# Transposing the gated product of three SwiGLU FFNs by DMA, as two planes of 16 bits, in place of TensorE

## The chip, the cores and the metric

The kernel runs on one core of a Trainium2 chip. The metric is the device time of one execution in microseconds (us): the median of three runs, 1262.65 us (1261.54 to 1262.88). One further execution was recorded by the hardware profiler; all durations below come from that one. Its span is 1259.9 us, and its granted TensorE clock 0.998 of full speed. Lines (L...) are those of the kernel before, unless the changed kernel is named.

## What is computed

Two layers over 256 latent tokens of width 1024, with 256 context tokens run through the same weights. Layer 0 is half-step FFN, neighbourhood attention, half-step FFN; layer 1 is half-step FFN, short gated convolution, half-step FFN. The last three FFNs, which the change concerns, work on the latent tokens alone. The output is the latent stream. All weights are float32.

```python
def swiglu_ffn(h, w_in, w_out):                 # w_in 1024 x 5632, w_out 2816 x 1024
    a, u = jnp.split(h @ w_in, 2, axis=-1)
    return (jax.nn.silu(a) * u) @ w_out

def half_step_ffn(x, shift, scale, gate, w_in, w_out, g, b):
    y = swiglu_ffn(modulate(x, shift, scale), w_in, w_out)
    return post_norm_update(x, y, gate, 0.5, g, b)   # layer_norm(alpha * x + 0.5 * gate * y)
```

shift, scale and gate come from a matrix-vector product of the condition c with `ada_w` (9 vectors per layer).

## The kernel before

**Precision.** A float32 product is made of three matmul passes over operands that are split in a high part (`...h`, rounded to the matmul's format) and a low part (`...l`, the remainder): high by high, low weights by high, high by low (`mmu`, L160 to 167; the rows L164, L165 and L167 of the profile are the three). ScalarE makes the high part by a copy, VectorE the low part by a subtraction.

**Weights.** A weight unit is 512 KB. `wunit` (L179) has SyncE (SP) load it into a raw tile (`w1r` for the first GEMM of an FFN, two DMAs of 256 KB; `w2r` for the second, one DMA of 512 KB; 4 raw buffers), ScalarE copies the high part in two halves of 128x512 (L210) and VectorE subtracts the low part in two halves (L213). High and low tiles have 5 buffers, and from the second phase on `ext[0]` more (L195 to 201): 3, so 8 units can be split ahead of their last use by TensorE. SP, ScalarE, VectorE and GpSimd each work through their own queue in a fixed order that a scheduler writes when the program is built; TensorE's order is written out by hand. An instruction that waits holds up all that stands behind it on its queue.

**An FFN.** `ffn` (L825) runs 11 panels (`panels`, L449). A panel is 256 gate columns and 256 up columns: 4 weight units, each used for both token tiles (t = 0, 1), so 8 steps on TensorE. Each step ends with `tick` (L143), which counts steps, runs the work whose due step has come (`Late`), and starts background work: the ada vectors of layer 1, in pieces of one DMA of 512 KB (`ar`, L303) and VectorE multiply-adds (`acc`, L296), at a rate of 0.35 per step in the first of the three FFNs, 0.25 in the second, 0.15 in the third.

When a panel's sums for one tile are done, `done` in `gated` (L475) has ScalarE write Silu of the gate half out of PSUM to `sil` (128x256, L478) and VectorE multiply it in place by the up half (L479). Rows of `sil` are tokens; the second GEMM needs columns of tokens. So at t == 1 a `Late` of `G_LAG = 4` steps follows: TensorE transposes four blocks of 128x128 (L487) into a PSUM bank `gT`, and `finish` splits that bank into `gh` on ScalarE (L112) and `gl` on VectorE (L113).

The second GEMM (`out_gemm`) runs 22 units `w2r`, tile 1 trailing tile 0 by 5 units (`order_skew`, L493), and ends in LayerNorm; the next FFN's or mixer's first units are loaded and split meanwhile.

**Where they lie.** The three FFNs take about 592 to 780 us, 781 to 965 us and 1065 to 1253 us of the span; in each the panels are the first 120 us or so, the second GEMM the rest. The first FFN of the kernel (both streams, L679), the attention and the short convolution are not touched; the convolution calls `gated` too (`uT`) and keeps its transposes on TensorE.

Of the kernel before, what the change touches and what calls it, by code (L numbers as in the profile page):

```python
# [8 lines left out]

F32 = mybir.dt.float32  # L10
F32R = mybir.dt.float32r
AF = mybir.ActivationFunctionType
ALU = mybir.AluOpType
AX = mybir.AxisListType
# [2 lines left out]
P = 128  # L17
# [34 lines left out]
LT_LAG = (5, 5)  # L52
F0_LAG = (5, 5, 6, 7)
G_LAG = 4
ROPE_EARLY = 70
S_EARLY = 40
V_LAG = 1
# [13 lines left out]
def backbone_kernel(  # L71
# [6 lines left out]
    nc = tc.nc  # L78
    sync = nc.sync
# [4 lines left out]
    sp = ctx.enter_context(tc.tile_pool(name="sp", bufs=2))  # L84
# [3 lines left out]
    hp = phase.__enter__()  # L88
# [3 lines left out]
    ext = [1, 0]  # L92
    ada_late = [0]

    def nm(s):
        uid[0] += 1
        return f"{s}_{uid[0]}"

    def act(dt=F32, s="a"):
        return ap.tile([P, 512], dt, tag="act", name=nm(s))  # L100
# [4 lines left out]
    def mmb(s="mm", t=0):  # L105
        return bank("at" if t % 2 else "mm", s)

    def tpb(s="tp"):
        return bank("tp", s)

    def split(src, hi, lo):
        a = nc.scalar.activation(hi, src, AF.Copy)  # L112
        return a, nc.vector.tensor_tensor(out=lo, in0=src, in1=hi.bitcast(F32), op=ALU.subtract)  # L113
# [42 lines left out]
    def drain():  # L156
        while background[0] is not None:
            bg_step()
# [20 lines left out]
    def wunit(srcs, kn, s, own=None, wd=512, put_off=False):  # L179
# [4 lines left out]
        if own:  # L184
            hs, ls = ([act(F32R, s + c) for _ in range(kn)] for c in "hl")
            rv = raw[:, :kn * 512].rearrange("p (a b) -> p a b", a=kn)
            with tc.high_priority(offset=w_early[0]):
                for src, c in srcs:
                    sync.dma_start(rv[:, :, c:c + src.shape[2]], src)
                for i in range(kn):  # L190
                    with queued(own[i]):
                        nc.scalar.activation(hs[i], rv[:, i], AF.Copy)
                        nc.vector.tensor_tensor(out=ls[i], in0=rv[:, i], in1=hs[i].bitcast(F32), op=ALU.subtract)
            return Parts(hs), Parts(ls)
        ext[1] += 1  # L195
        if ext[0] and ext[1] % (5 + ext[0]) in (E0 if ext[0] == 1 else E2):
            hi = hp.tile([P, UN], F32R, tag="whx", bufs=ext[0], name=nm(s + "h"))
            lo = hp.tile([P, UN], F32R, tag="wlx", bufs=ext[0], name=nm(s + "l"))
        else:
            hi = wp.tile([P, UN], F32R, tag="wh", bufs=WB[1], name=nm(s + "h"))  # L200
            lo = wp.tile([P, UN], F32R, tag="wl", bufs=WB[2], name=nm(s + "l"))
        rv, hv, lv = (t[:, :kn * wd].rearrange("p (a b) -> p a b", a=kn) for t in (raw, hi, lo))
# [4 lines left out]
        def parts():  # L207
            m = kn * wd
            for a in range(0, m, m // W_HI):
                nc.scalar.activation(hi[:, a:a + m // W_HI], raw[:, a:a + m // W_HI], AF.Copy)  # L210
            for a in range(0, m, m // W_LO):
# [35 lines left out]
    nc.scalar.dma_start(crow[8:16], c_ctx.rearrange("(a b) -> a b", b=P))  # L247
    nc.scalar.activation(warm, warm, AF.Silu)
    b0 = [[mmb("f0", z) for z in range(2)] for _ in range(3)]
# [8 lines left out]
    nc.tensor.transpose(pt[:, 0:16], crow, ident[0:16, 0:16])  # L258
    nc.scalar.activation(cst[:, :, 0:2], pt[:, 0:16].rearrange("p (v k) -> p k v", v=2), AF.Silu)
    nc.vector.memset(ones, 1.0)  # L260
# [114 lines left out]
    def queued(ins):  # L375

        es = ExitStack()
        for i in ins:
            es.enter_context(tc.issue_after(i.ins))
        return es  # L380
# [29 lines left out]
    def modulated(z, mv, rs, GB, lag, ahead=False):  # L410
# [4 lines left out]
        def rest():  # L415
            G, B = GB.get()
            res = []
            for h in range(2):
# [4 lines left out]
                with tc.high_priority(offset=LN_EARLY):  # L423
                    hi, lo = act(F32R, "hTh"), act(F32R, "hTl")
                    for k in range(4):
                        s, c = slice(k * P, (k + 1) * P), slice(4 * h + k, 4 * h + k + 1)
                        nc.scalar.activation(t[:, s], ps[:, s], AF.Identity, bias=B[:, c], scale=G[:, c])
                    ins = split(t, hi, lo)
# [13 lines left out]
    def lead_in(np):  # L442

        r = range(KU)
        o = [(0, 0, u) for u in r] + [(0, 1, u) for u in r[:2]] + [(1, 0, u) for u in r] + [(1, 1, u) for u in r[:2]]
        o += [(t, 1, u) for u in r[2:] for t in range(2)]
        return o + [(t, p, u) for p in range(2, np) for u in r for t in range(2)]

    def panels(cols, w, hTs, order, done, s, own=()):  # L449


        units, banks = {(0, u): x for u, x in enumerate(own)}, {}
        for t, p, u in order:
            if (p, u) not in units:
                with ExitStack() as st:
                    for i in fence if p == 1 else first_mv if own and p == 0 else ():
                        st.enter_context(tc.issue_after(i))
                    units[p, u] = wpair(w, u, *cols[p], s)
            if (t, p) not in banks:
                banks[t, p] = mmb(s, t)  # L460
            hi, lo = units[p, u]
            mmu(banks[t, p], [(*hsl(hTs[t], UK * u + i), hi[:, i], lo[:, i]) for i in range(UK)], u == 0, u == KU - 1)
            if u == KU - 1:
                done(p, t, banks.pop((t, p)))
            yield
            tick()

    def run(gen):
        for _ in gen:
            pass  # L470

    def gated(func, finish, s):

        part, res = {}, []

        def done(p, t, bk):
            g = sp.tile([P, 256], F32, tag="s2", bufs=S2, name=nm("sil"))
            nc.scalar.activation(g, bk[:, 0:256], func)  # L478
            gate_ins[:] = [nc.vector.tensor_tensor(out=g, in0=g, in1=bk[:, 256:512], op=ALU.mult)]  # L479
            part[p, t] = g  # L480
            if t == 1:
                def rest():
                    ps = tpb(s)
                    for i in range(2):
                        g = part.pop((p, i))
                        for j in range(2):
                            nc.tensor.transpose(ps[:, j * 256 + i * P:j * 256 + (i + 1) * P], g[:, j * P:(j + 1) * P], ident)  # L487
                    return finish(p, ps)
                res.append(Late(G_LAG, rest))

        return done, res
# [209 lines left out]
    for q, (k0, n) in enumerate(steps):  # L701
        nxt = start_step(*steps[q + 1]) if q < 4 else iter(())
        for g in range(6 * n):
# [3 lines left out]
            if k < KC - 1:  # L707
                z, part = ZP[g % 6]
# [16 lines left out]
    for fh, (p0, p1) in enumerate(parts):  # L725
        gT = []
# [90 lines left out]
    def lhs_T(tl):  # L817
        def f(k, t):
            s = (k % 2) * 256 + t * P
            g = tl[k // 2]  # L820
            hi, lo = g.get() if isinstance(g, Late) else g
            return hi[:, s:s + P], lo[:, s:s + P]
        return f

    def ffn(hTs, later, l, j, i, gm, nxt, own=()):  # L825
        def finish(p, ps):
            hi, lo = act(F32R, "gh"), act(F32R, "gl")
            split(ps, hi, lo)
            return hi, lo

        done, gT = gated(AF.Silu, finish, "gT")

        def done2(p, t, bk):
            done(p, t, bk)
            if p == 1 and t == 1:
                later()

        run(panels([(p * 256, FF + p * 256) for p in range(NP)], ffn_w_in[l, j], hTs, lead_in(NP), done2, "w1", own))
        drain()
        g, hTs, later = sub_end(ffn_w_out[l, j], lhs_T(gT), 2 * NP, l, i, gm, 0.5, nxt, "w2",  # L840
                                order_skew(NP) if nxt else order_last(NP))
        run(g)
        return hTs, later
# [45 lines left out]
    def tile_panel(c0, c1, hl, s, each):  # L889

        units = []
        for t, hT in enumerate(hl):
            bk = mmb(s)
            for u in range(KU):
# [4 lines left out]
                if u == KU - 1:  # L899
                    with tc.high_priority(offset=ROPE_EARLY):  # L900
                        each(t, bk)
# [124 lines left out]
    hp = phase.__enter__()  # L1026
# [35 lines left out]
    for i in range(len(steps) + LAG + V_LAG):  # L1062
# [14 lines left out]
        n = int(credit)  # L1077
# [12 lines left out]
        j = i - LAG - V_LAG  # L1090
# [15 lines left out]
    phase = tc.tile_pool(name="ph2", bufs=1)  # L1106
    hp = phase.__enter__()
    bias_rows.clear()
    ext[0] = 3

    set_background(stream([(1, 4, 0), (1, 5, 0)]), 0.35, HOLD)
    hTs, later = ffn(hTs, later, 0, 1, 2, 8, (1, 0), own)
# [15 lines left out]
    w = sc_w_in[0]  # L1128
# [22 lines left out]
    def done(p, t, bk):  # L1151
        if p >= 2:
            return cdone(p, t, bk)
        b = sp.tile([P, 512], F32, tag="s2", bufs=S2, name=nm("bs"))
        nc.scalar.activation(b, bk, AF.Copy)
        bs[p, t] = b
        if t == 1:
            for j in range(2):
                def rest(j=j):
                    ps = tpb("bT")  # L1160
                    for i in range(2):
                        for t in range(2):
                            nc.tensor.transpose(ps[:, i * 256 + t * P:i * 256 + (t + 1) * P],
                                                bs[p, t][:, (2 * j + i) * P:(2 * j + i + 1) * P], ident)
                    b = act(F32, "bT")
                    nc.scalar.activation(b, ps, AF.Copy)
                    return b
                bT[2 * p + j] = Late(G_LAG, rest)
            if p == 1:
                later()  # L1170
# [3 lines left out]
    g, hTs, later = sub_end(sc_w_out[0], lhs_T(yT), KC, 1, 1, 5, 1.0, (1, 6), "wo", order_late(KU))  # L1174
# [57 lines left out]
```

## Time and profile before

| | |
|---|---|
| runs, median (lowest, highest) | 1262.65 us (1261.54, 1262.88) |
| span of the profiled execution | 1259.9 us |
| TensorE (PE) busy | 1245.4 us, 99% |
| VectorE (DVE) busy | 952.5 us, 76% |
| ScalarE (ACT) busy | 589.9 us, 47% |
| GpSimd (POOL) busy | 41.4 us, 3% |
| moved by DMA | 268.59 MB, mean 213 GB/s |

The median of the runs is 2.75 us above the span of the profiled execution. PE is the row of the matmuls themselves; the loads of their stationary operand (PEld) run beside it. Busy time of PE counts overlapping matmuls as they were pipelined, so what a matmul costs in time is read from the start of one to the start of the next. In rows of groups the columns are: line, engine, operation, tiles written and read, shapes, count, then busy us in all and mean ns of one, then the idle time before them with what ended it.

### The profile page before, as it was taken

How to read it: one execution, taken by the hardware profiler on the slowest of the kernel's cores; microseconds unless marked ns; L12 is line 12 of the kernel's file. 1: busy time of each engine (PE TensorE's matmuls, PEld its weight loads, DVE VectorE, ACT ScalarE, POOL GpSimd, SP SyncE). 2: the span in 40 equal slices, each digit the busy share in tenths (PEclk: the TensorE clock that was granted, in tenths of full speed). 3: DMA queues.
4: the chain of work that ended last, by engine and by line, in shares of the span. 5: the costliest groups of instructions: out<-in, count | busy, mean ns of one | idle time of the engine just before them, and what ended most of it. 6: DMA issues, size and time to landing. Idle time of an engine off the chain costs nothing.

```text
span 1259.9 us, 17303 instructions
## 1 busy us (share of the span) xinstructions
PE 1245.4 (99%) x5922; PEld 1007.2 (80%) x5922; DVE 952.5 (76%) x1678; ACT 589.9 (47%) x1152; POOL 41.4 (3%) x71
## 2 busy tenths in 40 slices
PE   9999999999999999999999999999999999999997
PEld 6787778777878877877888788888788887888786
DVE  3699987888878877889898546988546788876546
ACT  2432132312326456687655435655435644655431
POOL 0000000000001011121000000000000000000000
PEclk9999999999999999999999999999999999999999
DMA  9976678878842744465899645898645764886641
GB/s 300 310 241 215 197 239 280 269 255 266 300 149 85 217 93 92 93 130 170 256 342 318 225 144 169 285 340 268 214 145 170 247 202 131 262 289 184 223 158 55
DMA packets 202776, 268.59 MB, mean 213 GB/s; under 512 B 30090, under 2 KB 149362, under 8 KB 202688
## 3 DMA queue, kind: packets, MB, share of 16 engines
q1 hardware_dynamic: 202652, 267.48, 67.3%
q8 instruction: 46, 0.75, 0.2%
q14 instruction: 42, 0.34, 0.1%
q10 hardware_dynamic: 36, 0.02, 0.0%
HBM read 265.27 MB, written 2.17 MB: 212 GB/s over the span
## 4 chain that ended last, share of the span: by engine, by line
PE 92%; DVE 3%; ACT 3%; issue 1%; DMA 0%; POOL 0%; DVEq 0%; SPq 0%; ACTq 0%; POOLq 0%
PE f L679 19%; PE w L164 17%; PE w L167 17%; PE w L165 17%; PE wkv L164 2%; PE wkv L165 2%; PE wkv L167 2%; PE wc L164 2%; PE wc L167 2%; PE wc L165 2%; PE gT L487 1%; PE ada L608 1%; PE ada L327 1%; PE S L971 1%; ACT pr L979 1%
## 5 line engine op out<-in xcount | busy, mean ns | idle before, releaser
L210 ACT ACTIVATE w1h<-w1r 128x512 fp32r<-128x512 f32 (+1 forms) x352 | 199.8, 620 | 180.4 <-DMA w1r<-in_ffn_w_in_dram 73.3
L213 DVE TENSOR_TENSOR w1l<-w1r,w1h 128x512 fp32r<-128x512 f32 (+1 forms) x352 | 222.9, 679 | 44.6 <-ACT w1h L210 43.3
L164 PE MATMUL w<-w1h,hTh 128*128 128x512 f32 x528 | 209.4, 397 | 0.9 <-ACT hTh L112 0.9
L165 PE MATMUL w<-w1l,hTh 128*128 128x512 f32 x528 | 206.0, 390 | 0.2 <-DVE w1l L213 0.2
L296 DVE SCALAR_TENSOR_TENSOR acc<-ar,cst,acc 128x512 f32<-128x512 f32 x266 | 186.0, 746 | 15.4 <-DMA ar<-in_ada_w_dram 15.4
L164 PE MATMUL w<-w2h,gh 128*128 128x512 f32 (+1 forms) x446 | 173.4, 389 | 0.0
L165 PE MATMUL w<-w2l,gh 128*128 128x512 f32 (+1 forms) x446 | 172.1, 386 | 0.0
L213 DVE TENSOR_TENSOR w2l<-w2r,w2h 128x512 fp32r<-128x512 f32 x176 | 114.3, 688 | 76.0 <-ACT w2h L210 75.2
L210 ACT ACTIVATE w2h<-w2r 128x512 fp32r<-128x512 f32 x176 | 101.6, 624 | 146.0 <-PE w L167 103.6
L167 PE MATMUL w<-w1h,hTl 128*128 128x512 f32 x528 | 163.2, 390 | 0.3 <-DVE hTl L113 0.2
L167 PE MATMUL w<-w2h,gl 128*128 128x512 f32 (+1 forms) x446 | 136.1, 386 | 0.0
L679 PE MATMUL f<-h0h,w1h 128*128 128x512 f32 x352 | 133.3, 394 | 0.4 <-DVE h0h L634 0.4
L679 PE MATMUL f<-h0l,w1h 128*128 128x512 f32 x352 | 133.2, 391 | 0.0
L679 PE MATMUL f<-h0h,w1l 128*128 128x512 f32 x352 | 132.7, 390 | 0.0
L164 PEld LDWEIGHTS w<-w1h,hTh 128*128 128x128 f32 x528 | 99.2, 188 | 23.8 <-ACT hTh L112 1.7
L167 PEld LDWEIGHTS w<-w1h,hTl 128*128 128x128 f32 x528 | 98.9, 188 | 22.4 <-DVE hTl L113 1.5
L165 PEld LDWEIGHTS w<-w1l,hTh 128*128 128x128 f32 x528 | 99.2, 188 | 20.2 <-DVE w1l L213 0.6
L164 PEld LDWEIGHTS w<-w2h,gh 128*128 128x128 f32 x446 | 83.8, 188 | 19.2 <-issue 1.7
L165 PEld LDWEIGHTS w<-w2l,gh 128*128 128x128 f32 x446 | 83.8, 188 | 16.6
L167 PEld LDWEIGHTS w<-w2h,gl 128*128 128x128 f32 x446 | 83.3, 188 | 17.1
L679 PEld LDWEIGHTS f<-h0h,w1h 128*128 128x128 f32 x352 | 65.9, 189 | 18.8 <-issue 4.2
L679 PEld LDWEIGHTS f<-h0l,w1h 128*128 128x128 f32 x352 | 65.6, 188 | 14.3 <-issue 0.6
(186 smaller groups left out, 1684.5 us busy)
## 6 DMA issues: line engine op xcount, KB each, us to landing
w1r<-in_ffn_w_in_dram SPq DMA_DIRECT2D x340, 256.0 KB
ar<-in_ada_w_dram SPq DMA_DIRECT2D x128, 512.0 KB
w2r<-in_ffn_w_out_dram SPq DMA_DIRECT2D x88, 512.0 KB
ar<-in_ada_w_dram SPq DMA_DIRECT2D x32, 256.0 KB
wkvr<-in_na_w_qkv_dram SPq DMA_DIRECT2D x32, 256.0 KB
wcr<-in_sc_w_in_dram SPq DMA_DIRECT2D x32, 256.0 KB
wqr<-in_na_w_qkv_dram SPq DMA_DIRECT2D x8, 512.0 KB
wor<-in_na_w_out_dram SPq DMA_DIRECT2D x8, 512.0 KB
```

Of the source, the lines that this page charges most:

```text
L164: nc.tensor.matmul(ps, lh, rh, start=first and i == 0, stop=False)
L165: nc.tensor.matmul(ps, lh, rl, start=False, stop=False)
L167: nc.tensor.matmul(ps, ll, rh, start=False, stop=last and i == n - 1)
L210: nc.scalar.activation(hi[:, a:a + m // W_HI], raw[:, a:a + m // W_HI], AF.Copy)
L213: nc.vector.tensor_tensor(out=lo[:, a:b], in0=raw[:, a:b], in1=hi[:, a:b].bitcast(F32), op=ALU.subtract)
L296: nc.vector.scalar_tensor_tensor(out=a, in0=src, scalar=sc, in1=a, op0=ALU.mult, op1=ALU.add)
L327: nc.tensor.matmul(ps[32 * j:32 * j + 32, :], ones, acc[i][h], start=True, stop=True)
L487: nc.tensor.transpose(ps[:, j * 256 + i * P:j * 256 + (i + 1) * P], g[:, j * P:(j + 1) * P], ident)
L608: nc.tensor.matmul(ps[o:o + 32, 0:m], cst[:, a * kt + i, :], w[:, i, j, :], start=(a == 0 and i < 2), stop=(a == last and i >= kt - 2))
L679: nc.tensor.matmul(ps, w, hT0[k][part == 1], start=(k == part == 0), stop=(k == KC - 1 and part == 1))
L971: nc.tensor.matmul(banks[i], (qh, qh, ql)[f][ps, qs], (kh, kl, kh)[f][ps, :], start=f == 0, stop=f == 2)
L979: nc.scalar.activation(pr, S, AF.Exp, bias=mx[:, 0:1], accum_out=mx[:, 1:2])
```

## The change

In the three FFNs of the second phase (`by_dma`), per panel and tile: behind the gate multiplication ScalarE copies the product, read as 16-bit halves, into a tile `hal` with all low halves in one plane and all high halves in the other (128x512 elements of 16 bits, 2 buffers; L486 of the changed kernel). SP issues one transposing DMA from `hal` to half of `halT` (4 blocks of 128x128 of 16 bits, 128 KB; 2 buffers; L487 there). At t == 1 a `Late` of `D_LAG = 8` steps follows: ScalarE joins the two planes into a float32 tile `gTw` in SBUF (1024 elements of 16 bits per partition; L491 there), and the same `finish` splits `gTw` (L114 and L115 there) instead of a PSUM bank. The room for the new tiles comes from the split weights: `ext[0]` goes from 3 to 2, so 7 units instead of 8 can be split ahead.

In counts: 132 transposes leave TensorE; 66 copies and 33 joins are added on ScalarE, 66 transposing DMAs on SP. The splits of `gT`, 33 on ScalarE and 33 on VectorE, stay in number.

```diff
+D_LAG = 8
...
-    def gated(func, finish, s):
+    def gated(func, finish, s, by_dma=False):
...
             g = sp.tile([P, 256], F32, tag="s2", bufs=S2, name=nm("sil"))
             nc.scalar.activation(g, bk[:, 0:256], func)
             gate_ins[:] = [nc.vector.tensor_tensor(out=g, in0=g, in1=bk[:, 256:512], op=ALU.mult)]
+            if by_dma:
+                if t == 0:
+                    part[p] = hp.tile([P, 4, 256], U16, tag="halT", bufs=2, name=nm("halT"))
+                halves = hp.tile([P, 2, 256], U16, tag="hal", bufs=2, name=nm("hal"))
+                nc.scalar.activation(halves, g.bitcast(U16).rearrange("p (f s) -> p s f", s=2), AF.Copy)
+                sync.dma_start_transpose(part[p][:, :, t * P:(t + 1) * P], halves.rearrange("p s f -> p (s f)"))
+                if t == 1:
+                    def joined():
+                        w = sp.tile([P, 512], F32, tag="tmp", bufs=3, name=nm("gTw"))
+                        nc.scalar.activation(w.bitcast(U16).rearrange("p (f s) -> p s f", s=2),
+                                             part.pop(p).rearrange("p (s j) n -> p s (j n)", s=2), AF.Copy)
+                        return finish(p, w)
+                    res.append(Late(D_LAG, joined))
+                return
             part[p, t] = g
...
-        done, gT = gated(AF.Silu, finish, "gT")
+        done, gT = gated(AF.Silu, finish, "gT", True)
...
-    ext[0] = 3
+    ext[0] = 2
```

The order on ScalarE in the panels of the first of the three FFNs, before, from one split of a transposed product (`gh<-gT`) to the next. `w1h` is the high part of a weight unit, `sil` the activated gate half; numbers behind names are running numbers of tiles.

```order
L112 ACTIVATE gh_1165_6232<-gT_1164_6227 128x512
L210 ACTIVATE w1h_1207_6440<-w1r_1206_6439 128x512 x2
L210 ACTIVATE w1h_1214_6474<-w1r_1213_6473 128x512 x2
L478 ACTIVATE sil_1175_6286<-w1_1159_6198 128x256
L478 ACTIVATE sil_1176_6295<-w1_1160_6205 128x256
L210 ACTIVATE w1h_1217_6495<-w1r_1216_6494 128x512 x2
L210 ACTIVATE w1h_1223_6526<-w1r_1222_6525 128x512 x2
L112 ACTIVATE gh_1187_6345<-gT_1186_6340 128x512
```

The same stretch of ScalarE's queue in the changed kernel, from one join to the next:

```order
L491 ACTIVATE gTw_1187_6303<-halT_1160_6182 128x2x512
L114 ACTIVATE gh_1188_6305<-gTw_1187_6303 128x512
L212 ACTIVATE w1h_1218_6439<-w1r_1217_6438 128x512 x2
L212 ACTIVATE w1h_1225_6467<-w1r_1224_6466 128x512 x2
L480 ACTIVATE sil_1184_6296<-w1_1171_6217 128x256
L486 ACTIVATE hal_1186_6300<-sil_1184_6296 128x512
L480 ACTIVATE sil_1190_6315<-w1_1172_6224 128x256
L212 ACTIVATE w1h_1229_6492<-w1r_1228_6491 128x512 x2
L486 ACTIVATE hal_1191_6318<-sil_1190_6315 128x512
L212 ACTIVATE w1h_1232_6513<-w1r_1231_6512 128x512 x2
L491 ACTIVATE gTw_1212_6420<-halT_1185_6299 128x2x512
```

The first `hal` stands directly behind its `sil`, whose VectorE multiplication lies between them; the second has the two halves of one weight unit between. From the second `hal` to the join of the same panel (`halT_1185`) there stand the two halves of one weight unit.

SP's queue in that stretch, before: loads of weight units and of ada pieces alone.

```order
L205 DMA w1r_1199_6411<-in_ffn_w_in_dram 128x2x256 x2
L205 DMA w1r_1206_6439<-in_ffn_w_in_dram 128x2x256 x2
L205 DMA w1r_1213_6473<-in_ffn_w_in_dram 128x2x256 x2
L303 DMA ar_1171_6267<-in_ada_w_dram 128x1024
L303 DMA ar_1181_6314<-in_ada_w_dram 128x1024
L205 DMA w1r_1216_6494<-in_ffn_w_in_dram 128x2x256 x2
```

SP's queue there in the changed kernel, with the two transposes of one panel:

```order
L207 DMA w1r_1217_6438<-in_ffn_w_in_dram 128x2x256 x2
L487 DMA_TRANSPOSE halT_1160_6182<-hal_1161_6183 128x4x128
L207 DMA w1r_1224_6466<-in_ffn_w_in_dram 128x2x256
L487 DMA_TRANSPOSE halT_1160_6182<-hal_1166_6201 128x4x128
L305 DMA ar_1180_6277<-in_ada_w_dram 128x1024
L305 DMA ar_1196_6337<-in_ada_w_dram 128x1024
```

Each transpose waits on SP for its `hal`, and the loads behind it wait with it. The order of the matmuls themselves is the same in both kernels, without the four `gT` transposes between two steps.

More of the change, by code (lines that the diff above doesn't have):

```diff
@@ L11 @@
 F32R = mybir.dt.float32r
+U16 = mybir.dt.uint16
 AF = mybir.ActivationFunctionType
```

## The prediction, made before the changed kernel ran

> **What bounds the kernel now.** I read first the page's chain of the work that ended last, to see which engine an edit must touch to move the end.
>
> ```profile
> span 1259.9 us, 17303 instructions
> PE 92%; DVE 3%; ACT 3%; issue 1%; DMA 0%; POOL 0%; DVEq 0%; SPq 0%; ACTq 0%; POOLq 0%
> PE f L679 19%; PE w L164 17%; PE w L167 17%; PE w L165 17%; PE wkv L164 2%; PE wkv L165 2%; PE wkv L167 2%; PE wc L164 2%; PE wc L167 2%; PE wc L165 2%; PE gT L487 1%; PE ada L608 1%; PE ada L327 1%; PE S L971 1%; ACT pr L979 1%
> ```
>
> TensorE carries 92% of the chain, and the transposes of the product (`gT L487`) stand on it themselves. Then I read the chain in order of time inside a panel (start, length, what), to price them where they stand.
>
> ```profile
> 642.72 0.46 PE w L167 x2
> 643.17 0.44 PE gT L487 x4
> 643.61 0.24 PE w L164
> ...
> 654.07 0.46 PE w L167 x2
> 654.53 0.44 PE gT L487 x4
> ```
>
> One panel is 654.53 − 643.17 = 11.36 us, of which the four transposes delay the next matmul by 0.44 us; nothing in it waits. Without them TensorE needs 10.92 us. Third, the busy times by stretch: start and end, then busy us of PE, PEld, DVE, ACT and POOL, the clock, the DMA share and GB/s. The first is early in the panels of the first FFN, the second later in them, the third its second GEMM, the last the third FFN's panels.
>
> ```profile
> 620.00:640.00 20.00, 20.00 (x93) 16.55 (x93) 17.56 (x31) 10.45 (x20) 0.00 (x0) 1.00 0.81 274
> 640.00:660.00 20.00, 20.00 (x93) 16.54 (x93) 20.00 (x35) 11.35 (x23) 0.00 (x0) 1.00 0.98 336
> 740.00:760.00 20.00, 20.00 (x90) 16.55 (x89) 12.57 (x21) 8.07 (x14) 0.00 (x0) 1.00 0.59 198
> 1120.00:1140.00 20.00, 20.00 (x93) 16.55 (x92) 15.56 (x26) 10.58 (x20) 0.00 (x0) 1.00 0.70 217
> ```
>
> TensorE is full in all, but VectorE and the DMA engines are full too at 640 us (20.00 of 20; 0.98). ScalarE has 8.65 us of 20 free there, which is what the change spends. What protects TensorE is the stock of split weight units. The groups by line give it, from 585 us to 611 us and to 660 us: one unit is two ScalarE halves and four matmuls of L164.
>
> ```profile
> L210 ACT ACTIVATE w1h<-w1r 128x512 fp32r<-128x512 f32 x19 | 11.0, 646 | 7.0 <-POOL rs L403 3.0 <-PE wo L167 1.9 <-DMA w1r<-in_ffn_w_in_dram 1.2
> L164 PE MATMUL w<-w1h,hTh 128*128 128x512 f32 x26 | 10.3, 398 | 0.2 <-ACT hTh L112 0.2
> ...
> L164 PE MATMUL w<-w1h,hTh 128*128 128x512 f32 x94 | 37.3, 397 | 0.2 <-ACT hTh L112 0.2
> ...
> L210 ACT ACTIVATE w1h<-w1r 128x512 fp32r<-128x512 f32 x58 | 33.4, 631 | 26.6 <-DMA w1r<-in_ffn_w_in_dram 13.8 <-PE w L167 4.7 <-DVE w1l L213 3.1
> ```
>
> By 611 us, where the first `gT` stood, 9.5 units are split and 6.5 used: 3 ahead; by 660 us 29 and 23.5: 5.5 ahead. A unit is two steps, 10.92 / 4 = 2.73 us. One unit is in hand, so the reserve at the first transpose is about 2 x 2.7 = 5.4 us.
>
> **The change part by part.** *TensorE's transposes go.* 33 groups of 0.44 us are 14.5 us, all on the chain. The row of the matmuls themselves says otherwise, and must not be used:
>
> ```profile
> L487 PE MATMUL gT<-ident,sil x132: 270/272/273, 611.6 to 1196.3; 128*128 128x128 f32 x132
> ```
>
> Each lasts 272 ns, but four start within 0.44 us, 110 ns apart. The Trainium skill ("TensorE: Matmul & The Clock Gate", Part 4: PE-mode transpose) gives some 275 ns for a transpose in a kernel's context. By it, taken as a price each, 132 would give 36.3 us and a forecast 21.8 us lower; the trace agrees with the duration, not with such a price. I take −14.5 us, also the most that can be won.
>
> *ScalarE's new work.* Rows of the first FFN's panels, ScalarE and VectorE:
>
> ```profile
> L210 ACT ACTIVATE w1h<-w1r 128x512 fp32r<-128x512 f32 x76 | 43.5, 628 | 32.3 <-PE w L167 14.4 <-DMA w1r<-in_ffn_w_in_dram 13.5 <-DVE w1l L213 3.1
> L478 ACT ACTIVATE sil<-w 128x256 f32<-128x256 f32 x21 | 7.9, 381 | 10.7 <-PE w L167 10.7
> L112 ACT ACTIVATE gh<-gT 128x512 fp32r<-128x512 f32 x10 | 5.9, 591 | 3.3 <-PE gT L487 3.3
> L479 DVE TENSOR_TENSOR sil<-sil,w 128x256 f32<-128x256 f32 x21 | 8.6, 416 | 3.3 <-ACT sil L478 3.3
> L296 DVE SCALAR_TENSOR_TENSOR acc<-ar,cst,acc 128x512 f32<-128x512 f32 x28 | 19.5, 745 | 0.0
> L213 DVE TENSOR_TENSOR w1l<-w1r,w1h 128x512 fp32r<-128x512 f32 x78 | 49.5, 686 | 10.1 <-ACT w1h L210 10.0
> ```
>
> No row shows a 16-bit copy. A `hal` has the 512 elements of a half unit: 0.63 us. Between 256 and 512 elements ScalarE takes (628 − 381) / 256 = 0.96 ns each, so a join of 1024 takes 0.63 + 512 x 0.96 ns = 1.12 us. Should 16 bits go at half the price, both are 0.3 and 0.6; at double, 1.25 and 2.2; I take the rows' rate, as the instructions are otherwise copies of the same kind. `gh` then reads SBUF, 0.63 for 0.59.
>
> *The path that matters* is ScalarE's queue around the join. Work per panel: four units (two halves start to end take 1.15 us, row below) 4.60, two `sil` 0.76, two `hal` 1.26, join 1.12, `gh` 0.63: 8.37 us, under 10.92, so the work alone fits. To it come two waits. The first `hal` stands directly behind its `sil`, so ScalarE waits for VectorE's 0.42 us, or 1.17 with an `acc` of 0.75 ahead of it: 0.8. And it waits at the join for the transpose: T from the end of the second `hal`, less what stands between (one unit in the rows shown, 1.15; two and a half at the place before it, 2.9; middle 2.0). So a panel takes ScalarE 8.37 + 0.8 + T − 2.0 = 7.2 + T.
>
> *T* is shown by no row. Bounds from issues of plain DMAs and what waited for them:
>
> ```profile
> 990.40 0.93 SPq L345 DMA_DIRECT2D lng<-in_ln_g_dram  x2
> 996.23 1.90 DVE L780 TENSOR_TENSOR x<-x,lng 128x512 f32<-128x512 f32 x3 [2.15 <-DMA lng<-in_ln_g_dram]
> 1256.41 0.99 SPq L812 DMA_DIRECT2D out_dram<-x  x2
> ```
>
> With an empty queue, the end of the span comes 1259.9 − 1257.4 = 2.5 to 3.5 us after the last store's issue; behind weight loads, 996.23 − 991.33 = 4.9 to 5.8 us pass. So T is 2.5 to 5.8 if a transpose is like a plain DMA. At DMA shares of 0.81 to 0.98 it is nearer to the second row: I take 4.4 in the first two FFNs, 3.8 in the third (share 0.70). Then ScalarE's panel is 11.6 and 11.0 us against 10.92. Ten intervals between joins cost 10 x 0.68 − 5.4 = 1.4 us in each of the first two FFNs, nothing in the third: +2.8. At T = 2.5 it is 0; at 5.8, (10 x 2.08 − 5.4) x 3 = 46 us.
>
> *The queues.* Behind a transpose on SP stand the next loads; each waits until `hal` is written. Beside the waits of ScalarE on loads this counts:
>
> ```profile
> ACT w1h L210 <- DMA w1r<-in_ffn_w_in_dram: 10.1, 6, 3.8
> ...
> ACT w1h L210 <- PE w L167: 14.4, 12, 1.6
> ```
>
> At 610 to 640 us loads come late (10.1 us in all), at 640 to 700 us buffers bound (14.4): so the reserve fills only after the first panels. The transposes add 2 x 128 KB per panel; at 336 GB/s that is 0.78 us of engines that are full at 640 us. Over four such panels in each of two FFNs that is 6.2 us, or nothing where the wait at the join covers it: half, +3.1.
>
> *FFN ends.* In the changed order a `hal` stands once per FFN ahead of the next split on the way, at most 0.63 x 3 = +1.9.
>
> *Seven units instead of eight.* In the second GEMM (ScalarE by time):
>
> ```profile
> 733.02 1.15 ACT L210 ACTIVATE w2h<-w2r 128x512 fp32r<-128x512 f32 x2 [1.59 <-PE w L167]
> 735.74 1.15 ACT L210 ACTIVATE w2h<-w2r 128x512 fp32r<-128x512 f32 x2 [1.57 <-PE w L167]
> ```
>
> A split starts when TensorE frees a buffer, every 2.72 us. Tile 1 trails by five units, so six are held and two are ahead: 5.4 − 1.15 (ScalarE) − 0.69 (VectorE) = 3.6 us of slack; with seven, 2.72 − 1.84 = 0.9. I cost it at nothing: what hides it is that ScalarE has little else (8.07 of 20). One `acc` of 0.75 in front is still covered; two are not.
>
> Sum: −14.5 + 2.8 + 3.1 + 1.9 = −6.7 us. The profiled span with the 2.75 us around it is the median, so 1262.65 − 6.7 = 1256.0 us.
>
> **The rivals.** *All is hidden.* T is 3 or so: ScalarE needs 10.2 us and never falls behind. Then 1262.65 − 14.5 = 1248.2, with FFN ends 1250. For it: ScalarE's free 8.65 us of 20. Against: shares of 0.98.
>
> *ScalarE's wait at the join sets the pace: slower.* It is the same cycle with T beyond some point, where 10 x (7.2 + T − 10.92) − 5.4 reaches the 3.2 us per FFN that are left of the gain, (14.5 − 3.1 − 1.9) / 3: that is T = 4.6. T = 5 gives 7.4 us per FFN, 22 in all: 1262.65 − 14.5 + 22 + 5.0 = 1275; T = 5.8 gives 1299. For it: the 4.9 to 5.8 us of the `lng` row, and that ScalarE's weight splits, which feed TensorE, stand behind the join. Against: when TensorE is slowed, the loads thin out and T falls. Of this rival's chance a third, 0.10, is for T of 5.2 and more: 1281 and up. Beside this stands a rule of the Trainium skill ("VectorE: DVE Perf Modes", The three transpose paths): a 128x128 transpose by DMA takes 1309 ns, and TensorE is to be used where PSUM will do. An estimate from it, four blocks one behind the other, is 5.2 us for one DMA, and so a T of at least that; no row here tells.
>
> *The transposes clog the DMA engines.* If one holds the engines for the 2.5 us of the empty-queue row, two make 5 us a panel beside 0.81 x 11.36 = 9.2 in the first FFNs and 8.0 in the third. 14.2 and 13.0 us per panel give (33 − 5.4) x 2 + (21 − 5.4) = 71 us: 1320. Another page of the Trainium skill ("DMA: Bandwidth & Descriptors", Latency and other measured facts) speaks against this with 261 GB/s for transposing DMAs, by which 128 KB take 0.5 us (an estimate).
>
> *Seven buffers bite.* Two `acc` ahead of a split in the second GEMM exceed the 0.9 us by 0.6; on 1 to 5 units of each FFN that is 2 to 9 us on top of the forecast: 1258 to 1265. VectorE's 12.57 of 20 speak against more.
>
> That the change doesn't do what it says is excluded by the order of the instructions: the matmul groups of `gT` are gone and the transposes stand on SP.
>
> **How the numbers follow.** Forecast 0.33 (own range 1250 to 1261), all hidden 0.17, wait at the join 0.30, clogged 0.12, seven buffers 0.08. A measurement here tells 0.2% from no change, 2.5 us: faster is below 1260.1, slower above 1265.2. Faster: 0.17 + 0.27 of the forecast + 0.03 of the buffers = 0.47. Same: 0.05 + 0.04 + 0.03 of the join case = 0.12. Slower: 0.27 + 0.12 + 0.01 + 0.01 = 0.41. The range runs from 1247.5 (all hidden, less the runs' scatter) to 1285 (T = 5.3 at the join); left out are the clogged case, 0.12, and 0.08 of the join case's upper end.
>
> **What would show it.** Right: panels in the changed trace of 10.92 us on PE in the third FFN, and in the first two some steps in which PE waits for ACT or DVE splits; a join on ACT that idles 2 to 3 us for a DMA; `hal` near 0.63 and the join near 1.1 us; second GEMMs with no wait. Wrong: joins that idle over 4 us and panels above 11.4 us (the slower rival); a DMA share near 0.98 in the third FFN (clogged); PE waiting in the second GEMM (buffers); no wait anywhere (all hidden).

## The result, and the profile after

The changed kernel takes 1297.19 us (median of 4 runs, 1293.82 to 1299.21) against 1262.12 us before, of which there are now four runs: the ratio is 1.0276, with a 95% interval of 1.026 to 1.0291. It is slower by 35 us, where a gain of 6.7 us was forecast. The profiled execution has a span of 1295.7 us. Its page, the span and the chain of the work that ended last:

```profile
span 1295.7 us, 17199 instructions
...
PE 58%; DMA 15%; DVE 12%; ACT 9%; issue 4%; SPq 2%; POOL 0%; DVEq 0%; ACTq 0%
PE f L695 19%; PE w L167 8%; PE w L166 8%; PE w L169 7%; DMA w1r<-in_ffn_w_in_dram 7%; DMA halT<-hal 5%; DVE w1l L215 5%; ACT w1h L212 2%; PE wc L166 2%; PE wc L167 2%; PE wc L169 2%; DMA lng<-in_ln_g_dram 1%; DVE acc L298 1%; ACT gTw L491 
```

TensorE carried 92% of the chain before and carries 58% now; the transposing DMA alone has 5%. But that does not say in which stage the time went. For this I take each stage from the first to the last start of its matmuls of high weights by high, as the view by tile gives them. For the third FFN, before and after (the first row of each pair is the second GEMM, the second the panels):

```profile
L164 PE MATMUL w<-w2h,gh x94: 278/389/474, 1191.9 to 1252.0; 128*128 128x512 f32 x82, 128*128 128x256 f32 x12
L164 PE MATMUL w<-w1h,hTh x176: 389/389/499, 1064.9 to 1191.0; 128*128 128x512 f32 x176
```

```profile
L166 PE MATMUL w<-w2h,gh x94: 278/389/795, 1215.6 to 1287.5; 128*128 128x512 f32 x82, 128*128 128x256 f32 x12
L166 PE MATMUL w<-w1h,hTh x176: 389/389/499, 1093.5 to 1214.7; 128*128 128x512 f32 x176
```

The panels are 126.1 us before and 121.1 after: the full gain of the transposes is there. The second GEMM is 60.1 before and 72.0 after. All three FFNs, in us, and the runs that are told below:

| | panels 1 | panels 2 | panels 3 | second GEMM 1 | 2 | 3 | median us |
|---|---|---|---|---|---|---|---|
| before | 126.7 | 126.3 | 126.1 | 60.8 | 60.9 | 60.1 | 1262.12 |
| changed | 125.7 | 132.2 | 121.1 | 71.9 | 71.5 | 72.0 | 1297.19 |
| e1 seven units alone | 126.7 | 125.9 | 125.9 | 60.8 | 60.9 | 60.1 | 1262.14 |
| e2 no join waits | 124.5 | 124.9 | 121.1 | 61.8 | 60.4 | 59.6 | 1252.65 |
| e3 last two panels on TensorE | 133.3 | 141.0 | 129.3 | 60.9 | 60.9 | 60.1 | 1287.75 |
| e4 joins moved | 124.3 | 131.0 | 121.1 | 63.8 | 60.4 | 59.6 | 1261.88 |
| e5 last two joins don't wait | 125.0 | 132.0 | 121.1 | 63.1 | 64.6 | 67.6 | 1274.68 |
| e6 first nine joins don't wait | 123.6 | 124.3 | 121.1 | 70.0 | 71.3 | 59.6 | 1270.83 |
| e7 plain DMA | 121.9 | 125.9 | 121.1 | 67.1 | 69.1 | 62.6 | 1268.64 |
| e8 no waits, no DMA | 122.9 | 121.2 | 121.0 | 60.3 | 60.4 | 59.6 | 1246.19 |
| e9 third FFN alone, moved | 126.7 | 125.9 | 121.1 | 60.8 | 60.8 | 59.6 | 1256.55 |
| e10 first and third, moved | 123.8 | 125.9 | 121.1 | 63.8 | 60.8 | 59.6 | 1258.80 |
| e11 moved, issued by ScalarE | 122.1 | 121.1 | 121.1 | 65.3 | 61.9 | 59.6 | 1254.04 |
| e12 third FFN alone, not moved | 126.7 | 125.9 | 121.1 | 60.9 | 60.9 | 67.9 | 1265.20 |

From before to changed the panels together are 0.1 us shorter (−1.0, +5.9, −5.0) and the second GEMMs 33.6 us longer (11.1, 10.6, 11.9). The span grew by 35.8 us: nearly all of it is in the second GEMMs. That is the net change. Without the four transposes a panel would be 0.44 us shorter, some 4.8 us per FFN, so the panels of the second FFN lost about 11 us of their own (132.2, where e8 has 121.2). (In the kernel before, the second FFN runs to about 970 us, 908.7 + 60.9, and not to 965.)

Why there? ScalarE's queue by time, in the third FFN's panels of the changed kernel (start, length, and in brackets the idle time before with what ended it):

```profile
1157.19 0.63 ACT L486 ACTIVATE hal<-sil 128x512 uint16<-128x512 uint16 x1 [1.15 <-DVE sil L481]
1157.73 0.37 ACT L480 ACTIVATE sil<-w 128x256 f32<-128x256 f32 x1
1157.99 1.14 ACT L212 ACTIVATE w1h<-w1r 128x512 fp32r<-128x512 f32 x2
1159.04 0.62 ACT L486 ACTIVATE hal<-sil 128x512 uint16<-128x512 uint16 x1
1159.56 1.14 ACT L212 ACTIVATE w1h<-w1r 128x512 fp32r<-128x512 f32 x2
1163.18 1.37 ACT L491 ACTIVATE gTw<-halT 128x1024 uint16<-128x1024 uint16 x1 [2.48 <-DMA halT<-hal]
1164.58 0.63 ACT L114 ACTIVATE gh<-gTw 128x512 fp32r<-128x512 f32 x1
1165.12 2.18 ACT L212 ACTIVATE w1h<-w1r 128x512 fp32r<-128x512 f32 x4
1167.20 0.36 ACT L480 ACTIVATE sil<-w 128x256 f32<-128x256 f32 x1
1168.71 0.63 ACT L486 ACTIVATE hal<-sil 128x512 uint16<-128x512 uint16 x1 [1.15 <-DVE sil L481]
```

From one first copy to the next are 1168.71 − 1157.19 = 11.52 us, for TensorE's 10.92. Of these ScalarE waits 1.15 us for VectorE's multiplication and 2.48 us for the transpose; the work is 7.9 us. So ScalarE falls back by 0.6 us in this panel of the lightest FFN, and TensorE lives on the stock. The eight last intervals between first copies in this FFN are 11.2 to 12.8 us. How much of it is left when the second GEMM begins is counted by the halves of `w2` split by then, before (until 1191.9 us) and after (until 1215.6 us):

```profile
L210 ACT ACTIVATE w2h<-w2r 128x512 fp32r<-128x512 f32 x14 | 8.1, 624 | 8.5 <-PE w L167 8.5
```

```profile
L212 ACT ACTIVATE w2h<-w2r 128x512 fp32r<-128x512 f32 x4 | 2.2, 617 | 0.0
```

Seven units before, two after; the other two FFNs have the same counts, 14 halves and 4. And the second GEMM starts at double pace: tile 1 trails by five units, so for its first five units TensorE takes a new one every 1.36 us. The chain by time at that point of the changed kernel:

```profile
1217.50 0.62 ACT hal L486
1218.12 0.11 ACT w2h L212
1218.23 3.25 DMA halT<-hal
...
1221.56 1.35 ACT gTw L491
...
1229.00 0.53 ACT hal L486
...
1229.55 5.36 DMA halT<-hal
...
1234.93 1.35 ACT gTw L491
...
1236.84 0.62 ACT w2h L212
```

The joins of the tenth and eleventh panel stand here ahead of the splits that TensorE waits for, and each waits for its transpose (3.25 and 5.36 us of chain). In this GEMM the starts of matmuls that lie over 0.5 us apart add up to 9.1 us of standing, and those a little apart to 3.2 us more, which is the clock (last section).

### The profile page after: what moved, and what is told of

Its sections match the earlier page's. It is cut to its first block, busy times and chain, and to the rows that moved or that the text cites. A ratio compares the mean times of both kernels' runs of the same rounds, so it can differ in the third digit from the quotient of the medians.

```text
span 1295.7 us, 17199 instructions
## 1 busy us (share of the span) xinstructions
PE 1250.8 (97%) x5790; PEld 998.6 (77%) x5790; DVE 949.6 (73%) x1678; ACT 661.0 (51%) x1251; POOL 41.8 (3%) x71
## 4 chain that ended last, share of the span: by engine, by line
PE 58%; DMA 15%; DVE 12%; ACT 9%; issue 4%; SPq 2%; POOL 0%; DVEq 0%; ACTq 0%
PE f L695 19%; PE w L167 8%; PE w L166 8%; PE w L169 7%; DMA w1r<-in_ffn_w_in_dram 7%; DMA halT<-hal 5%; DVE w1l L215 5%; ACT w1h L212 2%; PE wc L166 2%; PE wc L167 2%; PE wc L169 2%; DMA lng<-in_ln_g_dram 1%; DVE acc L298 1%; ACT gTw L491 1%; PE wkv L166 1%
## 5 line engine op out<-in xcount | busy, mean ns | idle before, releaser
L166 PE MATMUL w<-w1h,hTh 128*128 128x512 f32 x528 | 206.7, 392 | 1.7 <-ACT hTh L114 0.9
L166 PE MATMUL w<-w2h,gh 128*128 128x512 f32 (+1 forms) x446 | 178.2, 400 | 16.7 <-ACT w2h L212 16.7
L167 PE MATMUL w<-w2l,gh 128*128 128x512 f32 (+1 forms) x446 | 177.8, 399 | 3.1 <-DVE w2l L215 3.1
L169 PE MATMUL w<-w2h,gl 128*128 128x512 f32 (+1 forms) x446 | 139.6, 395 | 0.0
L169 PEld LDWEIGHTS w<-w2h,gl 128*128 128x128 f32 x446 | 85.9, 194 | 17.9
L491 ACT ACTIVATE gTw<-halT 128x1024 uint16<-128x1024 uint16 x33 | 45.1, 1367 | 73.8 <-DMA halT<-hal 73.8
```

What stands on the lines that cost most here:

```text
L166: nc.tensor.matmul(ps, lh, rh, start=first and i == 0, stop=False)
L167: nc.tensor.matmul(ps, lh, rl, start=False, stop=False)
L169: nc.tensor.matmul(ps, ll, rh, start=False, stop=last and i == n - 1)
L491: nc.scalar.activation(w.bitcast(U16).rearrange("p (f s) -> p s f", s=2), part.pop(p).rearrange("p (s j) n -> p s (j n)", s=2), AF.Copy)
```

## The experiments

Theory H: the loss is the two join waits at the hand-over from the panels to the second GEMM. Rival B: it is the buffer that was given up. Rival D: it is the traffic of the transposes. Each ratio is to runs of the kernel before that belong to the experiment; their medians lie between 1261.55 and 1262.13 us. After the first four runs H had to be widened to theory L: all eleven joins put ScalarE back, and the sum is paid where units go at double pace.

**e1: seven units alone.** The kernel before with one edit.

```diff
-    ext[0] = 3
+    ext[0] = 2
```

> The kernel before with seven split units instead of eight, nothing else. Theory H (hand-over): in the changed kernel the joins of the last two panels, each waiting on ScalarE for its transpose, stand ahead of the first splits of the second GEMM's weights, and TensorE spends its stock there at one unit per 1.36 us; that costs about 11 us per FFN. Then seven units alone cost little: 1262 to 1265 us, second GEMMs of 60.8 to 62 us. Rival B (buffers): the one unit fewer is what TensorE lacks at the start of the second GEMM; then 1285 us or more here. Rival D (DMA load): the traffic of the transposes delays the weight loads; then as under H, 1262 to 1265.

Measured: 1262.14 us, ratio 0.9999 (0.999 to 1.0008). B falls for the kernel before: there the eighth unit is worth nothing (the stock at the second GEMM is six units, 12 halves, and nothing waits). Eight units in the changed kernel were not tried. Its stock of two stands far below the limit of seven, so the limit isn't what it lacks; that is argued, not shown.

**e2: joins that don't wait.** The product used is not the real one.

```diff
-    nc.scalar.activation(w.bitcast(U16).rearrange("p (f s) -> p s f", s=2),
-                         part.pop(p).rearrange("p (s j) n -> p s (j n)", s=2), AF.Copy)
+    nc.scalar.activation(w.bitcast(U16).rearrange("p (a b) -> p a b", a=4),
+                         ident.bitcast(U16).unsqueeze(1).to_broadcast([P, 4, 256]), AF.Copy)
```

> The changed kernel with the join reading a constant tile in place of the transposed one: copies, transposing DMAs and joins all still run, but no join waits for a transpose; the product used is not the real one. H: the second GEMMs fall from 72 to 61 to 62 us, the total to 1250 to 1262 us. B: 1285 us or more, as the buffers are still seven. D: 1290 us or more, as the traffic is the same.

Measured: 1252.65 us, ratio 0.9922 (0.9906 to 0.9938). The second GEMMs are 59.6 to 61.8 us. With the same traffic and the same seven units, 44.5 us of the changed kernel's 1297.19 are gone: traffic or buffers alone don't make the loss. Such a join also takes 1.04 instead of 1.37 us, and the scheduler places it earlier: no join stands behind the start of a second GEMM here, two do in the changed kernel. So this run doesn't yet part the wait from the place of the join; e4 does.

**e3: the last two panels transposed by TensorE.**

```diff
-            if by_dma:
+            if by_dma and p < NP - 2:
```

> The changed kernel with the last two panels of each FFN transposed by TensorE as before, the first nine by DMA. H: the second GEMMs are 61 to 62 us, the total 1262 to 1270 us. B: about as the changed kernel, 1290 us or more. D: 2 of 11 of the loss comes back, about 1290 us.

Measured: 1287.75 us, ratio 1.0206 (1.019 to 1.0223). H foretold the second GEMMs (60.9, 60.9, 60.1) and missed the total by 18 us above its band: now the panels are 8 us longer than in the changed kernel. The waits in the stretch of the first FFN, and those of the third:

```profile
ACT gTw L491 <- DMA halT<-hal: 16.9, 8, 3.2
PEld gT L503 <- DVE sil L481: 6.7, 1, 6.7
```

```profile
ACT gTw L491 <- DMA halT<-hal: 18.3, 7, 3.4
...
PEld gT L503 <- DVE sil L481: 5.5, 1, 5.5
```

TensorE comes to its transposes, four steps or 5.5 us behind the sums, and the product is not there for another 5.5 to 6.7 us (8.1 in the second FFN): `sil` stands on ScalarE behind the last waiting join and the splits after it. So ScalarE's lag has built up over nine panels, and comes out wherever TensorE first needs something fresh of it. H in its narrow form falls.

**e4: joins moved.** All work as in the changed kernel; each join is ordered behind the first copy of the next panel, the last one six steps later.

```diff
+                if t == 0:
+                    behind_ins[:] = [c]          # c: the copy to hal
...
+                        with tc.issue_after((behind_ins if p < NP - 1 else hi_ins)[0].ins):
...
-                    res.append(Late(D_LAG, joined))
+                    res.append(Late(D_LAG + (6 if p == NP - 1 else 0), joined))
```

> The changed kernel with the same work, and each join placed on ScalarE behind the first copy of the next panel (the last panel's behind several splits of the second GEMM), so that the transpose has landed when its turn comes. H: no join idles over 0.5 us, the second GEMMs are 61 to 62 us, the total 1248 to 1260 us. B: 1285 us or more. D: 1290 us or more.

Measured: 1261.88 us, ratio 0.9997 (0.9987 to 1.0006): 35 us come back by order alone. ScalarE by time in the third FFN's panels:

```profile
1129.84 0.63 ACT L488 ACTIVATE hal<-sil 128x512 uint16<-128x512 uint16 x1 [0.90 <-DVE sil L483]
1130.38 1.35 ACT L496 ACTIVATE gTw<-halT 128x1024 uint16<-128x1024 uint16 x1
...
1139.50 0.63 ACT L488 ACTIVATE hal<-sil 128x512 uint16<-128x512 uint16 x1 [2.08 <-DVE sil L483]
1140.04 1.35 ACT L496 ACTIVATE gTw<-halT 128x1024 uint16<-128x1024 uint16 x1
```

No join waits in any panel, as expected, though two or three joins per FFN still stand behind the start of the second GEMM; in the second and third FFN these cost nothing. So it is the wait that costs, not the place. Two expectations were missed. The total is 2 us above the band, since the second FFN's panels still have 131.0 us; e11 takes that up. And the first FFN's second GEMM has 63.8 us for 61 to 62; it starts with 4 halves of `w2` split, the third with 12.

**e5 and e6: which joins.** The join of e2 for some panels only; the other joins wait. The same limits hold as there.

```diff
+                        if p >= NP - 2:      # e5; e6: if p < NP - 2
```

> The changed kernel; only the joins of the last two panels of each FFN read a constant tile instead of the transposed one, so these two don't wait; the first nine do. Theory H (the two waits at the hand-over are the loss): second GEMMs of 61 to 62 us, total 1262 to 1268 us. Theory L (lag: each of the eleven joins puts ScalarE back by a part of its wait, and the sum is paid where the second GEMM takes units at double pace): the lag of nine panels stays, second GEMMs of 66 to 69 us, total 1275 to 1288 us.

> The changed kernel; the joins of the first nine panels read the constant tile and don't wait, those of the last two wait for their transposes. H: the loss at the hand-over stays, second GEMMs of 70 to 72 us, total 1285 to 1292 us. L: ScalarE reaches the hand-over with a full stock and two waits of 3 to 4 us take little of it, second GEMMs of 61 to 64 us, total 1253 to 1262 us.

Measured: e5 1274.68 us (ratio 1.0101, 1.0086 to 1.0116), e6 1270.83 us (1.0071, 1.0054 to 1.0087). Over e2 the waits of the first nine joins cost 22.0 us, those of the last two 18.2, all eleven 44.5. e5 lies at the lower edge of L's band, e6 between the two bands: neither theory is right alone. The FFNs differ: in the third the last two waits cost nothing by themselves (59.6) and the nine cost 8 us (67.6); in the first two the last two waits cost 8 to 11 us by themselves (70.0, 71.3 against 61.8, 60.4). The stock says why. Halves of `w2` split when the second GEMM begins, third FFN of e5, third FFN of e6, first FFN of e6:

```profile
L212 ACT ACTIVATE w2h<-w2r 128x512 fp32r<-128x512 f32 x4 | 2.3, 617 | 0.0
```

```profile
L212 ACT ACTIVATE w2h<-w2r 128x512 fp32r<-128x512 f32 x12 | 6.9, 622 | 6.3 <-PE w L169 6.3
...
L212 ACT ACTIVATE w2h<-w2r 128x512 fp32r<-128x512 f32 x7 | 4.1, 622 | 0.7 <-DMA w2r<-in_ffn_w_out_dram 0.6
```

With 12 halves the two waits are covered; with 7, where loads come late, they are not; with 4 the GEMM stands even without them (63.1 to 67.6 us in the three FFNs of e5, with 3 to 4 halves each).

**e7: a plain DMA in place of the transposing one.** The product is not transposed.

```diff
-                sync.dma_start_transpose(part[p][:, :, t * P:(t + 1) * P], halves.rearrange("p s f -> p (s f)"))
+                sync.dma_start(part[p][:, :, t * P:(t + 1) * P], halves.rearrange("p s (j f) -> p (s j) f", j=2))
```

> The changed kernel with a plain DMA of the same bytes from the two planes to the same tile, in pieces of 256 bytes, in place of the transposing one; the product is not transposed. If transposing itself makes the DMA slow, the time from the second copy to the join falls from 3.7 to 2.5 to 3 us and the total to 1265 to 1280 us. If it is the latency of any DMA behind weight loads, it stays at 3.4 to 3.9 us and the total at 1290 us or more.

Measured: 1268.64 us, ratio 1.0057 (1.0036 to 1.0077). From the end of the second copy to the start of the join are 3.33 us on average over the 33 panels (2.2 to 5.1), against 3.76 (2.4 to 5.6) in the changed kernel. SP's issues in the two, minimum, median and longest in ns, changed kernel first:

```profile
L487 SPq DMA_TRANSPOSE halT<-hal x66: 1188/1191/1998, 604.5 to 1229.5; - x66
```

```profile
L487 SPq DMA_DIRECT2D halT<-hal x66: 593/600/681, 603.4 to 1205.0; - x66
```

The total fell as the first band had it; T lies between the two bands. But these means hold joins that didn't wait, 4 and 10 of the 33, where ScalarE's own work sets the time. For the joins that did wait, T is 3.82 us with the transposing DMA and 3.12 with the plain one. Of that, 1.51 and 0.63 us pass until SP has issued, and from there to the join 2.31 and 2.49 us. So once issued, the transposing DMA is not slower here; it comes later, by 0.6 us at the issue and the rest in SP's queue. That 0.7 us of T give 28.6 us back is not shown to be T alone, since SP is free sooner for the loads and the scheduler also put more splits between copy and join.

**e8: no waits and no transposing DMA.** e2 with the line of the DMA taken out.

> As the run whose joins read a constant tile, and the transposing DMAs left out as well: copies and joins on ScalarE alone. If the traffic of the transposes and their place in SP's queue hold up the weight loads (panels of the second FFN 124.9 us there, 121.1 in the third), these fall to 121 to 122 us and the total from 1252.7 to 1244 to 1247 us. If it is ScalarE's added work or the seven buffers, they stay, 1250 to 1253 us.

Measured: 1246.19 us, ratio 0.9877 (0.9862 to 0.9892), as expected. The second FFN's panels fall from 124.9 to 121.2 us. ScalarE's waits on weight loads, e2 first, then e8:

```profile
ACT w1h L212 <- DMA w1r<-in_ffn_w_in_dram: 92.6, 50, 5.7
```

```profile
ACT w1h L212 <- DMA w1r<-in_ffn_w_in_dram: 47.0, 32, 4.0
```

So the copies and joins as such cost nothing that shows, and the transposes' DMAs cost about 6 us (6.5 by the medians, 5.7 by the two ratios), by their traffic or by their place in SP's queue.

**e9, e10, e12: which FFNs.**

```diff
-        done, gT = gated(AF.Silu, finish, "gT", True)
+        done, gT = gated(AF.Silu, finish, "gT", nxt is None)   # e9, e12; e10: j == 1
```

> The moved joins of the run before (each behind the first copy of the next panel), with the DMA transposes in the third FFN alone; the first two are transposed by TensorE as before. In that run the third FFN had panels of 121.1 us and a second GEMM of 59.6 us, against 126.1 and 60.1 before, and the first two together lost that gain again. If the FFNs add up, 1262 - 5.5 = 1256 to 1258 us. If something else is lost with the change (the buffers, the ends of FFNs), 1260 us or more.

> The same with the first and the third FFN. With moved joins the first FFN had 124.3 and 63.8 us against 126.7 and 60.8 before: +0.6. If the FFNs add up, 1256 to 1259 us, no better than the third alone.

> The change as it was, joins not moved, in the third FFN alone. There the changed kernel's panels gained 5.0 us and the second GEMM lost 11.9: if the FFNs add up, 1262 + 6.9 = 1267 to 1271 us.

Measured: e9 1256.55 us (ratio 0.9958, 0.9945 to 0.9972), e10 1258.80 (0.9977, 0.9966 to 0.9987), both as expected. e12 gives 1265.20 (1.0026, 1.0016 to 1.0036), 2 us below its band: the second GEMM loses 7.8 us there, not 11.9, and its last join waits 2.85 us, not 5.40; why is open. Even in the FFN with the least traffic, the change with unmoved joins loses. e9 and e12 differ in nothing but the order of the joins in one FFN. Halves of `w2` split when its second GEMM begins, e9 first:

```profile
L214 ACT ACTIVATE w2h<-w2r 128x512 fp32r<-128x512 f32 x12 | 7.0, 623 | 5.4 <-PE w L169 5.4
```

```profile
L212 ACT ACTIVATE w2h<-w2r 128x512 fp32r<-128x512 f32 x5 | 2.8, 617 | 0.0
```

The second GEMM takes 59.6 us with the one, 67.9 with the other.

**e11: joins moved, transposes issued by ScalarE.**

```diff
-                sync.dma_start_transpose(part[p]...
+                nc.scalar.dma_start_transpose(part[p]...
```

> Moved joins in all three FFNs, with the transposing DMAs issued by ScalarE instead of SP, so that no weight load stands behind one. If what is still lost (panels of 131 us in the second FFN) comes from loads held up in SP's queue, these panels fall to 122 to 126 us and the total from 1262 to 1250 to 1256 us. If the traffic itself delays the loads, they stay at 129 us or more. Against either: issuing takes 1.19 us each on SP; if it takes ScalarE as long, 2.4 us a panel, ScalarE needs about 11 us a panel without any wait and the total is 1262 us or more.

Measured: 1254.04 us, ratio 0.994 (0.9926 to 0.9953): faster than both kernels, by 8 and 43 us. Issuing does take ScalarE as long (1.21 us each), but the 1262 us or more expected in that case didn't come. ScalarE's waits on weight loads in the second FFN's panels, e4 first; below it the largest row of the waits of SP's transposes there; then e11:

```profile
ACT w1h L214 <- DMA w1r<-in_ffn_w_in_dram: 32.5, 17, 4.0
```

```profile
SPq L491 <- ACT hal L488: 24.5, 8, 5.4
```

```profile
ACT w1h L214 <- DMA w1r<-in_ffn_w_in_dram: 13.8, 12, 3.7
```

The second FFN's panels fall from 131.0 to 121.1 us with the same transposes. So the loads were late because they stood behind transposes on SP, not because of the traffic. In these panels SP's transposes waited 44 us in all for ScalarE (24.5 in the row shown), and issuing 22 of them took it another 26 us; which of the two held the loads more isn't parted. This is shown for the kernel with moved joins; for the changed kernel itself, where SP's transposes waited 48 us in these panels, it wasn't tried. The first FFN's second GEMM stays at 65.3 us. It starts with four halves of `w2` and its last join waits 2.95 us, which is the picture of the changed kernel; why its stock is so short here stays open.

## Why the prediction was wrong

- **The transposes' 14.5 us** were about right: the third FFN's panels are 5.0 us shorter, and with all else hidden (e8) the ratio of 0.9877 is 15.5 us.
- **ScalarE's work**: the copy was right, the join was not, 1.37 us for the 1.12 forecast:

```profile
L486 ACT ACTIVATE hal<-sil x66: 613/630/667, 603.8 to 1228.9; 128x512 uint16<-128x512 uint16 x66
...
L491 ACT ACTIVATE gTw<-halT x33: 1342/1368/1387, 614.8 to 1234.9; 128x1024 uint16<-128x1024 uint16 x33
```

- **T** was within its bounds, and the value taken (4.4 and 3.8) was above the measured 3.87, 3.70 and 3.71 in the three FFNs. **ScalarE's panel** was to be 7.2 + T: 10.7 for the 3.52 us of the panel shown, where 11.52 were measured. The 0.8 us are the join (+0.25), the first copy's wait (1.15 for 0.8, +0.35) and the one unit between copy and join, where the middle of one and two and a half was taken (+1.0); 0.7 us come off, since instructions of ScalarE overlap at their ends.
- **The step that failed** is the reserve: "10 x 0.68 − 5.4 = 1.4 us". It let the panels spend the stock of split units, took what was spent for free, and put the second GEMM's loss at nothing. The panels did spend it and lost nothing in the third FFN. But the second GEMM needs this stock. It was priced from rows of its steady state (a split every 2.72 us, ScalarE 8.07 of 20 busy), where nothing presses; its first five units go at 1.36 us, with two joins still to come on ScalarE's queue. Seven units stood ready before, two now, and the three second GEMMs lost 33.6 us. That the waits at the joins spend the stock, and that the stock is what the second GEMM lacks, is shown by e4, and by e9 beside e12: the same work with the joins moved leaves six units in the third FFN, and its second GEMM loses nothing.
- **The signs.** A join that idles 2 to 3 us, taken as a sign of the forecast, came (2.24 us on average). TensorE waiting in the second GEMM came too, but it was taken as a sign of too few buffers; e1 speaks against that reading.
- **Seven units, the ends of FFNs**: e1 shows no cost of the buffer, as forecast; the +1.9 us of the ends can't be told from the noise of the stages.
- **The queues** were named and sized at +3.1, too little: e2 against e8 gives about 6 us, e4 against e11 7 to 8 us, most of it in the second FFN's panels.
- **The rivals**: the wait at the join was the right mechanism and the wrong threshold. It was to decide from T = 4.6; it decided at 3.76, since the price falls due at the hand-over and not in the panels. The rule behind the rival (the Trainium skill, "VectorE: DVE Perf Modes", Rules for kernel authors: TensorE where PSUM will do) came out right for the changed kernel and not for e11, where the DMA path is 8 us faster than TensorE's. The price beside the rule did not come out: four blocks at 1309 ns one behind the other are 5.2 us, the estimate of the prediction, and here copy to join takes 3.76 us for all four, latency included. The clogged engines didn't come: the DMA share in the third FFN's panels was 0.82.

## What to carry to other kernels

A stock that is built up ahead of an engine isn't free to spend: find the next place where it is drawn faster than it is filled, and price the change there, from rows of that place. When a transfer is put between two operations of one in-order engine, place the second one where the transfer has landed anyway: moving the joins was worth 35 us at equal work. And look at what stands behind a DMA that waits for its source: issuing it from the engine that writes the source took 7 to 8 us off here.

## What was not expected of the hardware

The idle stretches cost more than their length, since the granted clock fell after them. Windows of the changed kernel (the number after the engines is the granted clock):

```profile
738.00:741.00 3.00, 1.01 (x4) 0.34 (x2) 0.94 (x4) 2.97 (x5) 0.00 (x0) 0.96 0.23 85
741.00:742.00 1.00, 0.28 (x2) 0.04 (x1) 0.96 (x5) 1.00 (x3) 0.00 (x0) 0.50 0.00 0
...
746.00:747.00 1.00, 1.00 (x4) 0.80 (x3) 0.00 (x0) 0.00 (x0) 0.00 (x0) 0.50 0.84 276
747.00:748.00 1.00, 1.00 (x5) 0.80 (x4) 0.28 (x1) 0.94 (x2) 0.00 (x0) 0.72 0.50 178
748.00:749.00 1.00, 1.00 (x6) 0.81 (x5) 1.00 (x2) 0.21 (x1) 0.00 (x0) 1.00 0.11 41
```

TensorE stood for 2.0 of the 3 us from 738 to 741 us, in one piece, and then ran at half clock until about 747.6 us, about 3 us lost. The Trainium skill ("TensorE: Matmul & The Clock Gate", Part 1: The HAM clock gate) says that an idle window of some 3.4 us halves the clock until a busy one has passed; the 0.50 here agrees, the 2.0 us of standing are shorter than such a window. A transposing DMA also takes SP twice as long to issue as a plain one of the same bytes (1.19 against 0.60 us).
